# One wide matmul for both parts of x: the joint product in the feature-major steps of a two-block network

## The chip, the cores and the metric

The kernel runs on one core of one Trainium2 chip. The metric is the device time of one execution in microseconds (us). Three runs of the kernel before took 2135.95, 2133.17 and 2133.64 us, median 2133.64. The profiled execution is a fourth one.

## The reference

Two blocks of two layers each work on 256 tokens of 1024 features, in float32. Cut to what matters here:

```
h = layer_norm(x)
for layer in 0, 1:                                   # first block
    proj = h @ w_in[layer]                           # 1024 -> 2048: pool input, q, k, v
    mix  = concat(pool_mixer(...), stick_breaking_attention(q, k, v)) @ w_out
    h    = layer_norm(ALPHA * h + mix)
    f    = swiglu(h) if layer == 0 else top2_of_8_experts(h)
    h    = layer_norm(ALPHA * h + f)
for layer in 0, 1:                                   # second block
    z   = rms_norm(x) @ w_in_2[layer]                # gated recurrence, 3 groups of attention, gates
    x   = x + (gated mix of both branches) @ w_out_2
    x   = x + square(relu(rms_norm(x) @ w_up_2)) @ w_down_2
return rms_norm(x)
```

`swiglu(x) = (silu(x @ wg) * (x @ wu)) @ wd`, with an inner width of 2816; the inner width of the last pair is 4096.

## The kernel before

**Two parts of every number.** TensorE works here on float32 numbers that are rounded to fewer bits (the type fp32r). To keep the accuracy, every operand is a sum of two such numbers, a high part and a low part: `xh`, `xl` for the activations, `whi`, `wlo` for the weights. A product is then three matmuls, whi·xh + whi·xl + wlo·xh (`mm3`, L216 to L227). The product of the two low parts is left out.

**The stream of weights.** All weights come in units of 128 partitions by 2048 numbers (1 MB), in the order in which they are used. A unit is loaded by SyncE's DMA queue into `raw` (`emit_dma`, L144), then `emit_split` makes its two parts: ScalarE writes the high part (`whi`, L166, 2048 columns), VectorE subtracts it from `raw` for the low part (`wlo`, L168, one instruction over 2048 columns). `take` hands out the next unit, and keeps three units split and eight or so loaded ahead. `raw`, `whi` and `wlo` come out of one pool of 13 slots, so a new `whi` can wait for the slot of a unit that TensorE is just done with. There is a second way to make the low part: for units at or behind `self.hold` it is cut into three pieces of 592, 784 and 672 columns (L176), which are put into a list, `self.fill`, and are emitted one at a time by `filler`.

**Two ways to multiply.** A product whose result has tokens on the partitions (`chunk_tok`, `tok_part`, the experts, `down`) holds x still and moves 512 columns of weights (L225 to L227). A product whose result has features on the partitions holds 128x128 weights still and moves the 256 tokens of x (L221 to L223). The second kind is `chunk_feat` (L275). One call makes 512 features: two units (j), four columns blocks of 128 features (c), four steps of the contraction (k), so 32 steps of three matmuls of 256 columns. Its results lie in two of the four PSUM banks of the pool `acc`, two blocks c to a bank, so that a call and the next one use different banks. When both units are done, ScalarE or VectorE takes the results out of PSUM, 512 columns at a time.

**Who calls it.** 44 calls of `chunk_feat`, 1408 steps:

- the mixer of the first block, twice per layer (q and k): 4
- the dense feed-forward network of layer 0 (`ffn`, L725), one for each 256 inner features but the first 256: 10
- the second block (`second`, L1115), per layer: one for the forget gates, one for the queries of the recurrence, six for queries and keys of the three attention groups: 16
- the "up" half of the second block's feed-forward network, per layer: 7, so 14

**Side work.** `pump` runs the next piece of each generator in `self.side` behind every second block c, so four times in a call. Attention, pooling and the recurrence (`hgrn`) are such generators. A piece puts matmuls on TensorE's queue and their followers on ScalarE's and VectorE's. They use four other banks, two of them of the pool `ms`. Every engine works through its queue in the order in which the program put it there; nothing overtakes.

Where a stage ends, `boundary` normalises the two halves of the tokens and multiplies each by the next stage's first two units at once.

Of the kernel before, what the change touches and what calls it, by code (L numbers as in the profile page):

```python
# [10 lines left out]
F32 = mybir.dt.float32  # L11
# [86 lines left out]
class Net:  # L98
# [176 lines left out]
    def chunk_feat(self, x):  # L275

        xh, xl = x
        out = [self.bank(), self.bank()]
        for j in range(2):
            w = self.take(1)[0]  # L280
            for c in range(4):
                o = out[c // 2][:, (c % 2) * T:(c % 2 + 1) * T]
                for k in range(4):
                    kt = 4 * j + k
                    self.mm3(o, xh[:, kt, :], xl[:, kt, :], w[0][:, k, c * P:(c + 1) * P],
                             w[1][:, k, c * P:(c + 1) * P], kt == 0 and c % 2 == 0, kt == 7,
                             w_stationary=True, skip_group_check=True)
                if c % 2 == 1:
                    self.pump()
        return out  # L290
# [144 lines left out]
    def run(self, stop=None):  # L435
# [4 lines left out]
        self.x = (self.main.tile([P, KT, T], F32R, name="xh"), self.main.tile([P, KT, T], F32R, name="xl"))  # L440
# [160 lines left out]
    def mixer(self, l, ps):  # L601
# [3 lines left out]
        with self.mixs:  # L605
# [12 lines left out]
            for j in range(2):  # L618
                ps = self.chunk_feat(self.x)
                nc.scalar.activation(q[:, 2 * j:2 * j + 2].rearrange("p c t -> p (c t)"), ps[0], AF.Identity,  # L620
                                     scale=0.125)
                nc.vector.tensor_copy(k[:, 2 * j:2 * j + 2].rearrange("p c t -> p (c t)"), ps[1])
                for c in (2 * j, 2 * j + 1):
                    self.side.append(self.stick_pair(c, q, k, pairs, work))
# [100 lines left out]
    def ffn(self, ps):  # L725
        nc, a, tc = self.nc, self.a, self.tc
        with tc.tile_pool(name="ffn", bufs=1) as pool, tc.tile_pool(name="ffnw", bufs=2) as work:
# [13 lines left out]
            self.side.append(first())  # L741
            for j in range(1, FF // 256):
                ps2 = self.chunk_feat(self.x)
                s = work.tile([P, 512], F32, name="s")
                nc.scalar.activation(s, ps2[0], AF.Silu)
                nc.vector.tensor_mul(s, s, ps2[1])
                h, l = (m[:, 2 * j:2 * j + 2].rearrange("p c t -> p (c t)") for m in hid)
                nc.scalar.activation(h, s, AF.Identity)
                nc.vector.tensor_sub(l, s, h.bitcast(F32))
# [136 lines left out]
    def experts(self, gate, rank, xt, rest, iota1, sums, end):  # L886
        nc, a, tc = self.nc, self.a, self.tc
        mm = nc.tensor.matmul
        with tc.tile_pool(name="moew", bufs=2) as work:
# [4 lines left out]
            def gather(p):  # L894
# [7 lines left out]
                for i in range(2):  # L902
                    for k in range(0, KT, 2):
                        if p:
                            yield
                        ps = self.ms.tile([P, 512], F32, name="ms") if p else self.bank()
                        for j in range(2):
                            for t in range(2):
                                mm(ps[:, j * T:(j + 1) * T], xt[i][:, t, (k + j) * P:(k + j + 1) * P],
                                   s[:, t].rearrange("p e s -> p (e s)"), start=j == 0 and t == 0, stop=t == 1,  # L910
                                   skip_group_check=True)
                        nc.scalar.activation(xg[i][:, k:k + 2].rearrange("p k s -> p (k s)"), ps, AF.Identity)
# [202 lines left out]
    def second(self, l, ps, stop=None):  # L1115
        nc, a, tc = self.nc, self.a, self.tc
        self.n_ahead = N_AHEAD - 1
        with tc.tile_pool(name="z", bufs=1) as pool, tc.tile_pool(name="zw", bufs=2) as work:
# [12 lines left out]
            ps = self.chunk_feat(self.x)  # L1131
            for i in range(2):
                c = slice(512 * i, 512 * i + 512)
                nc.scalar.activation(f[:, c], ps[i], AF.Sigmoid)
                nc.scalar.activation(k[:, c], ps[i], AF.Sigmoid, scale=-1.0)
            for h in range(4):
                c = slice(T * h, T * h + T)
                nc.vector.tensor_scalar(f[:, c], f[:, c], lb[:, 4 + h:5 + h], lb[:, h:h + 1], op0=OP.mult, op1=OP.add)
                nc.vector.tensor_scalar(k[:, c], k[:, c], lb[:, 4 + h:5 + h], None, op0=OP.mult)
            ps = self.chunk_feat(self.x)  # L1140
            for i in range(2):
                c = slice(512 * i, 512 * i + 512)
                nc.scalar.activation(q[:, c], ps[i], AF.Sigmoid)
                nc.vector.tensor_mul(q[:, c], q[:, c], ps[i])
# [9 lines left out]
            for g in range(3):  # L1154
                qk = []
                for i in range(2):
                    ps = self.chunk_feat(self.x)
# [40 lines left out]
        with tc.tile_pool(name="up", bufs=1) as pool, tc.tile_pool(name="upw", bufs=2) as work:  # L1198
# [13 lines left out]
            self.side.append(first())  # L1212
            for j in range(1, FF2 // 512):
                ps2 = self.chunk_feat(self.x)
                for i in range(2):
                    s = work.tile([P, 512], F32, name="s")
# [3 lines left out]
                    nc.scalar.activation(h, s, AF.Identity)  # L1220
                    nc.vector.tensor_sub(lo, s, h.bitcast(F32))
# [218 lines left out]
```

## Time and profile before

| | |
|---|---|
| median of the runs | 2133.64 us (2133.17 to 2135.95) |
| profiled execution, its own time | 2134.69 us |
| its span, first to last instruction | 2132.9 us |
| TensorE busy / its weight loads | 2104.6 us (99%) / 1824.6 us (86%) |
| VectorE / ScalarE / GpSimd busy | 1484.9 us (70%) / 1215.3 us (57%) / 76.6 us (4%) |
| mean granted TensorE clock | 0.994 of full speed |
| HBM read | 503.73 MB, 237 GB/s over the span |

The busy time of a matmul in the profile is longer than the time after which the next one starts (a 256-column one is 0.28 us long, and the next starts 0.12 us after it), so the rate is read from the starts in the timeline. TensorE is named PE there, its weight loads PEld, VectorE DVE, ScalarE ACT and GpSimd POOL. L and a number is a line of the kernel.

### The profile page before, as it was taken

The page shows a single profiled execution, that of the slowest core. Times are in us where ns is not written, and L with a number is a line of the kernel's source. Part 1 is how long each engine was busy: PE and PEld are TensorE (multiplying, and loading weights), DVE is VectorE, ACT ScalarE, POOL GpSimd, SP SyncE. Part 2 cuts the span into 40 slices and gives each one's busy share as a digit, 9 for nine tenths or more (in the row PEclk, how much of TensorE's full clock was granted, in tenths as well). Part 3 has the DMA queues.
Part 4 walks back from the last instruction along what each step waited for, and adds up shares of the span by engine and source line. Part 5 has one row for each costly group of instructions (what it writes and reads, how often), then busy time and mean ns, then how long its engine had stood idle before and what let it go on. Part 6 is the DMA issues. An engine that isn't in the chain of part 4 may idle for free. (4 is left out here: it accounts for less than half of the span.)

```text
span 2132.9 us, 28748 instructions
## 1 busy us (share of the span) xinstructions
PE 2104.6 (99%) x11853; PEld 1824.6 (86%) x11853; DVE 1484.9 (70%) x1308; ACT 1215.3 (57%) x1191; POOL 76.6 (4%) x88
## 2 busy tenths in 40 slices
PE   9999999999999999999999899999999999999998
PEld 7899988788888888888888799988998899988987
DVE  6465454798888989898898666667654566666643
ACT  4544446677777777777776535464543444555542
POOL 0000000000000000000000110200000011100000
PEclk9999999899999999999999999999999999999999
DMA  8275555699999999999998354444654654436551
GB/s 302 88 246 181 197 186 189 223 362 369 363 345 367 369 344 352 375 365 336 371 358 304 139 176 149 137 147 156 221 196 152 221 171 145 144 124 225 185 197 60
DMA packets 240510, 508.29 MB, mean 238 GB/s; under 512 B 9346, under 2 KB 57346, under 8 KB 240372
## 3 DMA queue, kind: packets, MB, share of 16 engines
q1 hardware_dynamic: 237120, 497.22, 67.4%
q0 software_dynamic: 2816, 8.56, 1.4%
q8 instruction: 95, 1.56, 0.3%
q10 hardware_dynamic: 436, 0.60, 0.1%
q14 instruction: 43, 0.35, 0.0%
HBM read 503.73 MB, written 1.05 MB: 237 GB/s over the span
## 5 line engine op out<-in xcount | busy, mean ns | idle before, releaser
L168 DVE TENSOR_TENSOR wlo<-raw,whi 128x2048 fp32r<-128x2048 f32 x463 | 1061.0, 2294 | 367.9 <-ACT whi L166 318.6
L166 ACT ACTIVATE whi<-raw 128x2048 fp32r<-128x2048 f32 x467 | 886.9, 1915 | 259.1 <-PE acc L226 81.6
L225 PE MATMUL acc<-whi,xh 128*128 128x512 f32 x1168 | 467.1, 400 | 2.2 <-ACT xh L350 2.1
L227 PE MATMUL acc<-whi,xl 128*128 128x512 f32 x1168 | 458.2, 392 | 0.5 <-DVE xl L351 0.5
L226 PE MATMUL acc<-wlo,xh 128*128 128x512 f32 x1168 | 456.3, 391 | 1.6 <-DVE wlo L163 0.9
L221 PE MATMUL acc<-xh,whi 128*128 128x256 f32 x1408 | 403.8, 287 | 0.0
L223 PE MATMUL acc<-xh,wlo 128*128 128x256 f32 x1408 | 398.3, 283 | 0.0
L222 PE MATMUL acc<-xl,whi 128*128 128x256 f32 x1408 | 398.2, 283 | 0.0
L225 PE MATMUL acc<-whi,hidh 128*128 128x512 f32 x696 | 272.7, 392 | 0.0
L226 PE MATMUL acc<-wlo,hidh 128*128 128x512 f32 x696 | 271.2, 390 | 0.0
L227 PE MATMUL acc<-whi,hidl 128*128 128x512 f32 x696 | 271.0, 389 | 0.0
L221 PEld LDWEIGHTS acc<-xh,whi 128*128 128x128 f32 x1408 | 269.9, 192 | 1.3
L222 PEld LDWEIGHTS acc<-xl,whi 128*128 128x128 f32 x1408 | 270.0, 192 | 0.7
L223 PEld LDWEIGHTS acc<-xh,wlo 128*128 128x128 f32 x1408 | 269.8, 192 | 0.0
L227 PEld LDWEIGHTS acc<-whi,xl 128*128 128x128 f32 x1168 | 219.7, 188 | 52.7 <-DVE xl L351 5.9
L225 PEld LDWEIGHTS acc<-whi,xh 128*128 128x128 f32 x1168 | 220.2, 189 | 47.9 <-ACT xh L350 5.3
L226 PEld LDWEIGHTS acc<-wlo,xh 128*128 128x128 f32 x1168 | 220.3, 189 | 46.1 <-DVE wlo L163 1.9
L227 PEld LDWEIGHTS acc<-whi,hidl 128*128 128x128 f32 x696 | 130.6, 188 | 27.8
L225 PEld LDWEIGHTS acc<-whi,hidh 128*128 128x128 f32 x696 | 130.8, 188 | 25.9
L226 PEld LDWEIGHTS acc<-wlo,hidh 128*128 128x128 f32 x696 | 130.8, 188 | 25.6
L350 ACT ACTIVATE xh<-tr 128x512 fp32r<-128x512 f32 x40 | 22.5, 596 | 77.8 <-PE tr L357 77.6
L970 ACT ACTIVATE hidh<-tr 128x512 fp32r<-128x512 f32 (+1 forms) x48 | 27.1, 564 | 64.3 <-PE tr L357 64.3
(313 smaller groups left out, 1607.6 us busy)
## 6 DMA issues: line engine op xcount, KB each, us to landing
raw<-in_moe_wd_dram SPq DMA_DIRECT2D x88, 1024.0 KB, 6.5
raw<-in_moe_wg_dram SPq DMA_DIRECT2D x80, 1024.0 KB, 7.0
raw<-in_moe_wu_dram SPq DMA_DIRECT2D x80, 1024.0 KB, 6.6
raw<-in_w_in_dram SPq DMA_DIRECT2D x74, 1024.0 KB, 5.5
raw<-in_w_up_dram SPq DMA_DIRECT2D x32, 1024.0 KB, 5.4
raw<-in_w_down_dram SPq DMA_DIRECT2D x32, 1024.0 KB, 5.0
raw<-in_w_out_dram SPq DMA_DIRECT2D x16, 1024.0 KB, 5.3
raw<-in_ffn_wg_dram SPq DMA_DIRECT2D x22, 512.0 KB, 4.2
```

What stands on the lines that cost most here:

```text
L166: self.nc.scalar.activation(hi, raw, AF.Identity)
L168: self.nc.vector.tensor_sub(lo, raw, hi.bitcast(F32))
L221: mm(out, wh, xh, start=start, stop=False, **kw)
L222: mm(out, wh, xl, start=False, stop=False, **kw)
L223: mm(out, wl, xh, start=False, stop=stop, **kw)
L225: mm(out, xh, wh, start=start, stop=False, **kw)
L226: mm(out, xh, wl, start=False, stop=False, **kw)
L227: mm(out, xl, wh, start=False, stop=stop, **kw)
L350: self.nc.scalar.activation(h, v, AF.Identity)
L970: nc.scalar.activation(h[:, :n], v, AF.Identity)
```

## The change

`chunk_feat` is replaced by `chunk_join`. The high and the low part of x now lie side by side in one tile `xx`, so that one matmul of 512 columns makes whi·xh into the first and whi·xl into the second half of a bank, and a second one of 256 columns adds wlo·xh to the second half. A block c has a bank of its own, and a call uses all four banks. The two halves are added when they leave PSUM: ScalarE copies the first half (256 columns), VectorE adds the second (`joined`).

In these calls the low parts of the weights are made in the three pieces (hold is 0 around `take`). What `fill` holds is emitted at the first unit; the pieces of the second unit's `take` come one ahead of each block's exit from PSUM. What follows the exit (silu, square, gates) is handed on as a function, and is emitted behind the next block's exit. At the start of both feed-forward networks the first piece of the generator `first` runs at once instead of at the next `pump`.

```diff
-    def chunk_feat(self, x):
-        xh, xl = x
-        out = [self.bank(), self.bank()]
+    def chunk_join(self, sink):
+        mm = self.nc.tensor.matmul
+        out = []
         for j in range(2):
+            hold, self.hold = self.hold, 0
             w = self.take(1)[0]
+            self.hold = hold
+            if j == 0:
+                self.after()
+                self.filler(len(self.fill))
             for c in range(4):
-                o = out[c // 2][:, (c % 2) * T:(c % 2 + 1) * T]
+                if j == 0:
+                    out.append(self.bank())
                 for k in range(4):
                     kt = 4 * j + k
-                    self.mm3(o, xh[:, kt, :], xl[:, kt, :], w[0][:, k, c * P:(c + 1) * P],
-                             w[1][:, k, c * P:(c + 1) * P], kt == 0 and c % 2 == 0, kt == 7,
-                             w_stationary=True, skip_group_check=True)
+                    cw = slice(c * P, (c + 1) * P)
+                    mm(out[c], w[0][:, k, cw], self.xx[:, kt].rearrange("p i t -> p (i t)"), start=kt == 0, stop=False,
+                       skip_group_check=True)
+                    mm(out[c][:, T:], w[1][:, k, cw], self.xx[:, kt, 0], start=False, stop=kt == 7,
+                       skip_group_check=True)
+                if j == 1:
+                    self.filler()
+                    late = sink(c, (out[c][:, :T], out[c][:, T:]))
+                    self.after()
+                    self.late = late
                 if c % 2 == 1:
                     self.pump()
-        return out
+        self.filler(len(self.fill))
+
+    def after(self):
+        late, self.late = self.late, None
+        if late is not None:
+            late()
+
+    def joined(self, dst, halves, scale=1.0):
+        self.nc.scalar.activation(dst, halves[0], AF.Identity, scale=scale)
+        if scale == 1.0:
+            self.nc.vector.tensor_add(dst, dst, halves[1])
+        else:
+            self.nc.vector.scalar_tensor_tensor(dst, halves[1], scale, dst, op0=OP.mult, op1=OP.add)
...
-        self.x = (self.main.tile([P, KT, T], F32R, name="xh"), self.main.tile([P, KT, T], F32R, name="xl"))
+        self.xx = self.main.tile([P, KT, 2, T], F32R, name="xx")
+        self.x = (self.xx[:, :, 0], self.xx[:, :, 1])
+        self.late = None
...
@@ the queries and keys of an attention group @@
-                    ps = self.chunk_feat(self.x)
+                    x = pool.tile([P, 4, T], F32, name="qa" if i == 0 else "ka", bufs=2)
+
+                    def sink(c, ps, x=x):
+                        self.joined(x[:, c], ps)
+
+                    self.chunk_join(sink)
                     if i == 1:
                         self.rotate(*qk[0], rope)
-                    x = pool.tile([P, 4, T], F32, name="qa" if i == 0 else "ka", bufs=2)
-                    for j in range(2):
-                        nc.scalar.activation(x[:, 2 * j:2 * j + 2].rearrange("p c t -> p (c t)"), ps[j], AF.Identity)
...
@@ the up half of the second block's feed-forward network @@
-            self.side.append(first())
+            f = first()
+            next(f)
+            self.side.append(f)
             for j in range(1, FF2 // 512):
-                ps2 = self.chunk_feat(self.x)
-                for i in range(2):
-                    s = work.tile([P, 512], F32, name="s")
-                    nc.scalar.activation(s, ps2[i], AF.Relu)
-                    nc.vector.tensor_mul(s, s, ps2[i])
+                s = []
+
+                def square(i, j=j, s=s):
+                    v = s[i]
+                    nc.vector.scalar_tensor_tensor(v, v, 0.0, v, op0=OP.max, op1=OP.mult)
                     h, lo = (m[:, 4 * j + 2 * i:4 * j + 2 * i + 2].rearrange("p c t -> p (c t)") for m in hid)
-                    nc.scalar.activation(h, s, AF.Identity)
-                    nc.vector.tensor_sub(lo, s, h.bitcast(F32))
+                    nc.scalar.activation(h, v, AF.Identity)
+                    self.fill.insert(1, lambda: nc.vector.tensor_sub(lo, v, h.bitcast(F32)))
+
+                def sink(c, ps, s=s, square=square):
+                    if c % 2 == 0:
+                        s.append(work.tile([P, 512], F32, name="s"))
+                    self.joined(s[-1][:, c % 2 * T:c % 2 * T + T], ps)
+                    return (lambda: square(c // 2)) if c % 2 else None
+
+                self.chunk_join(sink)
+            self.after()
+            self.filler(len(self.fill))
...
```

The other callers change in the same manner: the dense network gets a silu and a product as late functions, the recurrence its gates and its swish, the mixer's q and k are only joined. In the experts one copy is written as a pattern of 2 x 256 columns instead of 512.

**Where the order moves.** The first place is VectorE in the up half, layer 0 of the second block, second call. `s` is the result outside PSUM (two tiles by turns), `acc` a bank, `hidl` and `hidh` the parts of the squared result. Before:

```order
L168 TENSOR_TENSOR wlo_15058<-raw_14915,whi_15057 128x2048
L168 TENSOR_TENSOR wlo_15112<-raw_14917,whi_15111 128x2048
L1218 TENSOR_TENSOR s_15165<-s_15165,acc_15055 128x512
L1221 TENSOR_TENSOR hidl_14908<-s_15165,hidh_14907 128x512
L1218 TENSOR_TENSOR s_15170<-s_15170,acc_15056 128x512
L1221 TENSOR_TENSOR hidl_14908<-s_15170,hidh_14907 128x512
```

The same place in the changed kernel, from the second unit of the call on:

```order
L176 TENSOR_TENSOR wlo_14674<-raw_14514,whi_14673 128x592
L315 TENSOR_TENSOR s_14687<-s_14687,acc_14637 128x256
L176 TENSOR_TENSOR wlo_14674<-raw_14514,whi_14673 128x784
L315 TENSOR_TENSOR s_14687<-s_14687,acc_14646 128x256
L176 TENSOR_TENSOR wlo_14674<-raw_14514,whi_14673 128x672
L315 TENSOR_TENSOR s_14710<-s_14710,acc_14655 128x256
L1275 SCALAR_TENSOR_TENSOR s_14687<-s_14687 128x512
L1278 TENSOR_TENSOR hidl_14502<-s_14687,hidh_14501 128x512
L315 TENSOR_TENSOR s_14710<-s_14710,acc_14664 128x256
L1275 SCALAR_TENSOR_TENSOR s_14710<-s_14710 128x512
```

Four adds over 256 columns (L315) have come in between the pieces of the low part, and the fourth stands behind the square and the low part of the first half.

The second place is VectorE in the first unit of the query call of the second attention group (g = 1, layer 0). `att` is the recurrence's matrix, copied out of a bank of the pool `ms`; `w` holds the scores' maxima. Before:

```order
L168 TENSOR_TENSOR wlo<-raw,whi 128x2048
L1295 COPY_PREDICATED att_12887<-lev,ms 128x32x8
L1365 TENSOR_REDUCE w_13357<-ms 128x2
L1366 TENSOR_SCALAR w_13357<-w_13357 128x2
L1371 COPY ma<-w_13357 128x2
```

After:

```order
L176 TENSOR_TENSOR wlo<-raw,whi 128x592
L176 TENSOR_TENSOR wlo<-raw,whi 128x784
L176 TENSOR_TENSOR wlo<-raw,whi 128x672
L1362 COPY_PREDICATED att_12596<-lev,ms 128x32x8
L1432 TENSOR_REDUCE w_13026<-ms 128x2
```

Here only the low part is in pieces; the copy that frees the bank still stands behind all of it.

## Rows read from the trace of the kernel before

**Rows 1.** The page, parts 1 and 2: busy time, granted clock.

```profile
span 2132.9 us, 28748 instructions
PE 2104.6 (99%) x11853; PEld 1824.6 (86%) x11853; DVE 1484.9 (70%) x1308; ACT 1215.3 (57%) x1191; POOL 76.6 (4%) x88
PEclk9999999899999999999999999999999999999999
```

**Rows 2.** Waits of TensorE, longest first: us in total, times, longest us.

```profile
PE tr L418 <- DVEq L869: 4.0, 1, 4.0
PE tr L357 <- DVE r L432: 3.5, 2, 2.8
```

**Rows 3.** Windows, three calls: us; busy PE, PEld, DVE, ACT, POOL; clock; DMA; GB/s.

```profile
155.40:166.92 11.52, 11.52 (x99) 11.52 (x98) 5.97 (x4) 4.95 (x4) 0.00 (x0) 1.00 0.59 183
...
1358.43:1374.77 16.34, 16.34 (x137) 15.97 (x135) 9.42 (x19) 8.94 (x27) 3.62 (x5) 1.00 0.41 134
1515.52:1527.04 11.52, 11.52 (x99) 11.52 (x98) 7.28 (x7) 6.18 (x6) 0.00 (x0) 1.00 0.62 188
```

**Rows 4.** Timeline, TensorE, one call of the dense network: start, us, instruction.

```profile
155.40 0.28 PE L221 MATMUL acc<-xh,whi 128*128 128x256 f32 x1
...
166.92 0.28 PE L221 MATMUL acc<-xh,whi 128*128 128x256 f32 x1
```

**Rows 5.** Timeline, TensorE, 512-column matmuls of a token-major product, then a call.

```profile
1340.54 0.39 PE L225 MATMUL acc<-whi,xh 128*128 128x512 f32 x1
...
1341.90 0.28 PE L221 MATMUL acc<-xh,whi 128*128 128x256 f32 x1
```

**Rows 6.** Timeline, TensorE, among the experts: 256 columns between 512 and 512.

```profile
589.39 0.39 PE L227 MATMUL acc<-whi,hidl 128*128 128x512 f32 x1
589.62 0.64 PE L909 MATMUL ms<-slots,xtl 128*128 128x256 f32 x4
590.09 0.40 PE L225 MATMUL acc<-whi,hidh 128*128 128x512 f32 x1
```

**Rows 7.** The page, part 5: count, busy us, mean ns, idle before.

```profile
L221 PE MATMUL acc<-xh,whi 128*128 128x256 f32 x1408 | 403.8, 287 | 0.0
```

**Rows 8.** Groups by line and shape: count, busy us, mean ns, idle before.

```profile
L168 DVE TENSOR_TENSOR wlo<-raw,whi 128x2048 fp32r<-128x2048 f32 x463 | 1061.0, 2294 | 367.9 <-ACT whi L166 318.6 <-PE acc L226 22.5 <-issue 9.0
L166 ACT ACTIVATE whi<-raw 128x2048 fp32r<-128x2048 f32 x467 | 886.9, 1915 | 259.1 <-PE acc L226 81.6 <-PE acc L227 69.3 <-DVE wlo L168 57.5
L1218 DVE TENSOR_TENSOR s<-s,acc 128x512 f32<-128x512 f32 x28 | 19.1, 683 | 2.6 <-ACT s L1217 2.6
L1220 ACT ACTIVATE hidh<-s 128x512 fp32r<-128x512 f32 x28 | 17.7, 632 | 30.5 <-DVE s L1218 30.5
L991 DVE TENSOR_TENSOR hs<-hs,acc 128x256 f32<-128x256 f32 x8 | 3.3, 410 | 0.0
L989 ACT ACTIVATE hs<-acc 128x256 f32<-128x256 f32 x8 | 3.0, 376 | 0.0
```

**Rows 9.** One line, L176: the pieces; ns min/median/max, starts, forms.

```profile
L176 DVE TENSOR_TENSOR wlo<-raw,whi x6: 766/849/966, 402.8 to 1193.5; 128x592 fp32r<-128x592 f32 x2, 128x784 fp32r<-128x784 f32 x2, 128x672 fp32r<-128x672 f32 x2
```

**Rows 10.** Timeline, ScalarE in the up half; in brackets the idle time and what ended it.

```profile
1521.47 1.91 ACT L166 ACTIVATE whi<-raw 128x2048 fp32r<-128x2048 f32 x1 [1.91 <-PE acc L223]
```

**Rows 11.** Timeline, VectorE and TensorE, first unit of the group-1 query call.

```profile
1302.70 2.29 DVE L168 TENSOR_TENSOR wlo<-raw,whi 128x2048 fp32r<-128x2048 f32 x1 [5.77 <-ACT whi L166]
...
1304.91 0.42 DVE L1295 COPY_PREDICATED att<-lev,ms 128x256 f32<-128x256 uint8 x1
...
1305.39 1.10 PE L1292 MATMUL ms<-A,B 128*128 128x64 f32 x8
```

**Rows 12.** Timeline, the same engines, first unit of the group-2 key call.

```profile
1361.22 2.29 DVE L168 TENSOR_TENSOR wlo<-raw,whi 128x2048 fp32r<-128x2048 f32 x1 [1.82 <-ACT whi L166]
...
1364.98 1.12 DVE L1335 SCALAR_TENSOR_TENSOR y<-ms,rr,og 128x128 f32<-128x128 f32 x4 [1.16 <-POOL rr L1332]
...
1366.22 0.60 PE L357 MATMUL tr<-mats,y 128*128 128x128 f32 x4
```

More of the change, by code (lines that the diff above doesn't have):

```diff
@@ L739, in first, with silu, product, sink @@
                     self.split_to(hid, self.transpose4(hs[t], 2), 0, t, 2)
-            self.side.append(first())
+            f = first()
+            next(f)
+            self.side.append(f)
             for j in range(1, FF // 256):
-                ps2 = self.chunk_feat(self.x)
-                s = work.tile([P, 512], F32, name="s")
-                nc.scalar.activation(s, ps2[0], AF.Silu)
-                nc.vector.tensor_mul(s, s, ps2[1])
-                h, l = (m[:, 2 * j:2 * j + 2].rearrange("p c t -> p (c t)") for m in hid)
-                nc.scalar.activation(h, s, AF.Identity)
-                nc.vector.tensor_sub(l, s, h.bitcast(F32))
+                gs, us = (work.tile([P, 512], F32, name=n) for n in ("s", "u"))
+                def silu(s=gs):
+                    nc.scalar.activation(s, s, AF.Silu)
+                def product(j=j, s=gs, u=us):
+                    h, l = (m[:, 2 * j:2 * j + 2].rearrange("p c t -> p (c t)") for m in hid)
+                    nc.vector.tensor_mul(s, s, u)
+                    nc.scalar.activation(h, s, AF.Identity)
+                    self.fill.insert(1, lambda: nc.vector.tensor_sub(l, s, h.bitcast(F32)))
+                def sink(c, ps, gs=gs, us=us, late=(None, silu, None, product)):
+                    self.joined((us if c > 1 else gs)[:, c % 2 * T:c % 2 * T + T], ps)
+                    return late[c]
+                self.chunk_join(sink)
                 if j == 6:
                     g, b = self.load_rows((a["ln2_g"][0], a["ln2_b"][0]))
+            self.after()
+            self.filler(len(self.fill))
             acc = self.down(hid, FF // P)
@@ L911, in gather @@
                                    skip_group_check=True)
[L912 removed]
+                        nc.scalar.activation(xg[i][:, k:k + 2], ps.rearrange("p (k s) -> p k s", k=2), AF.Identity)
             def turn(p):
@@ L1130, in second, with gates, swish, sink @@
             f = pool.tile([P, 4 * T], F32, name="C")
-            ps = self.chunk_feat(self.x)
-            for i in range(2):
+            sq = pool.tile([P, 4 * T], F32, name="D")
+            def gates(i):
                 c = slice(512 * i, 512 * i + 512)
[L1134 to L1141, printed above, removed]
-                c = slice(512 * i, 512 * i + 512)
-                nc.scalar.activation(q[:, c], ps[i], AF.Sigmoid)
-                nc.vector.tensor_mul(q[:, c], q[:, c], ps[i])
+                nc.scalar.activation(k[:, c], f[:, c], AF.Sigmoid, scale=-1.0)
+                nc.scalar.activation(f[:, c], f[:, c], AF.Sigmoid)
+                for h in (2 * i, 2 * i + 1):
+                    c = slice(T * h, T * h + T)
+                    nc.vector.tensor_scalar(k[:, c], k[:, c], lb[:, 4 + h:5 + h], None, op0=OP.mult)
+                    nc.vector.tensor_scalar(f[:, c], f[:, c], lb[:, 4 + h:5 + h], lb[:, h:h + 1], op0=OP.mult,
+                                            op1=OP.add)
+            def swish(i):
+                c = slice(512 * i, 512 * i + 512)
+                nc.scalar.activation(sq[:, c], q[:, c], AF.Sigmoid)
+                self.fill.insert(1, lambda: nc.vector.tensor_mul(q[:, c], q[:, c], sq[:, c]))
+            for dst, then in ((f, gates), (q, swish)):
+                def sink(c, ps, dst=dst, then=then):
+                    self.joined(dst[:, c * T:c * T + T], ps)
+                    return (lambda: then(c // 2)) if c % 2 else None
+                self.chunk_join(sink)
+            self.after()
+            self.filler(len(self.fill))
             og = pool.tile([P, 2, 512], F32, name="og")
@@ L1210, in first @@
                     self.split_to(hid, self.transpose4(hs[t]), 0, t)
-            self.side.append(first())
+            f = first()
+            next(f)
+            self.side.append(f)
             for j in range(1, FF2 // 512):
-                ps2 = self.chunk_feat(self.x)
-                for i in range(2):
-                    s = work.tile([P, 512], F32, name="s")
-                    nc.scalar.activation(s, ps2[i], AF.Relu)
-                    nc.vector.tensor_mul(s, s, ps2[i])
-                    h, lo = (m[:, 4 * j + 2 * i:4 * j + 2 * i + 2].rearrange("p c t -> p (c t)") for m in hid)
-                    nc.scalar.activation(h, s, AF.Identity)
-                    nc.vector.tensor_sub(lo, s, h.bitcast(F32))
+                s = []
+                def square(i, j=j, s=s):
+                    v = s[i]
+                    nc.vector.scalar_tensor_tensor(v, v, 0.0, v, op0=OP.max, op1=OP.mult)
+                    h, lo = (m[:, 4 * j + 2 * i:4 * j + 2 * i + 2].rearrange("p c t -> p (c t)") for m in hid)
+                    nc.scalar.activation(h, v, AF.Identity)
[5 more added lines that the diff above has]
+                    return (lambda: square(c // 2)) if c % 2 else None
+                self.chunk_join(sink)
+            self.after()
+            self.filler(len(self.fill))
             acc3 = self.down(hid, FF2 // P)
```

7 lines of the change are left out of this document (3 added, 4 removed).

## The prediction

> **What bounds the kernel now.** I began with the page's busy times and its line of granted clocks [rows 1]: TensorE is busy for 99% of the span, with the granted clock at nine tenths or full speed in every slice, while VectorE is at 70% and ScalarE at 57%. Next the waits of TensorE, the longest of which are 4.0 and 3.5 us [rows 2]: idle time can hardly be won here, only shorter matmul work. Next the windows [rows 3], since the change touches one kind of stage: a call of the dense network (first row) and one of the up half (last row) each have 11.52 us of TensorE work in 11.52 us, at clock 1.00, with a DMA share of 0.59 and 0.62 and VectorE at 5.97 and 7.28 us. So these calls are bound by TensorE, and neither the weights' transfer nor another engine stands close behind. Then the timeline of TensorE, from which the pace comes [rows 4 to 6]; the groups, for the durations on ScalarE and VectorE [rows 8, 9]; and last the places where side work leaves little room [rows 10 to 12].
>
> **The pace of a matmul.** A call starts at 155.40 and the next at 166.92 [rows 4]: 11.52 us for 96 matmuls of 256 columns, 0.1200 us each. Six matmuls of 512 columns go from 1340.54 to 1341.90 [rows 5]: 0.2267 us each. So two of 256 cost 0.2400 where one of 512 costs 0.2267, and what a matmul costs beside its columns is 2 × 0.1200 − 0.2267 = 0.0133 us. The question is whether this holds where the two widths alternate, as they will. Among the experts they do once [rows 6]: a 512-column one from 589.39 to 589.62 (0.23), four of 256 from 589.62 to 590.09 (0.47, or 0.118 each), then 512 again. No width pays for its neighbour there beyond the timeline's rounding. I take 0.2267 + 0.1200 = 0.3467 us for a step that took 0.3600.
>
> **What it removes.** Each step loses one matmul and 0.0133 us. The count of steps is that of L221, 1408 [rows 7]: 1408 × 0.0133 = 18.8 us. A call falls from 11.52 to 11.09 us. Columns and products are the same as before.
>
> **What it adds, and what hides it.** Per call, from [rows 8, 9]:
> - VectorE, low parts: a whole one is 2.29 us, three pieces 0.77 + 0.97 + 0.85 = 2.58. Two units: 5.17 where it was 4.59.
> - VectorE, four adds of 256 columns from a bank: 0.41 each, by the nearest row, L991: 1.64.
> - VectorE in the up half keeps its two squares (0.68 by L1218, which had the same width) and two low parts (0.68 likewise): 2.73. Together 9.54 of 11.09 us, 86%. The dense network: 5.97 + 0.58 + 1.64 = 8.2.
> - ScalarE: two high parts of 1.92, four copies of 256 columns at 0.38 (L989), two of 512 at 0.63 (L1220): 6.6 of 11.09.
>
> None of it is on TensorE, which is the cover. The cover is gone when a bank comes free too late: a call takes all four banks, so the next one's block c0 needs the first bank at once, c1 four steps (4 × 0.3467 = 1.39 us) later, and so on. A block is finished in the second unit, and its bank is needed again 12 steps, 4.16 us, after that: c0 is done 1.39 us after the half and needed at the end of the call.
>
> I walk through the up half, the heaviest. The high part of the second unit is what starts late: in the call that starts at 1515.52 ScalarE waits 1.91 us for TensorE (the slot of an older unit) and starts at 1521.47, when half the call is over [rows 10]. In the new call the half is at 5.55 us and that start at some 5.74, its end at 7.65. Then the first piece on VectorE to 8.42, and behind it the rest:
> - c0: done by TensorE at 6.93, copied 7.65 to 8.03, added by 8.83; needed at 11.09. Slack 2.3 us.
> - c1: the piece of 784 to 9.8, add by 10.2; needed at 12.48. Slack 2.3.
> - c2: the piece of 672, add by 11.45; needed at 13.87. Slack 2.4.
> - c3: done at 11.09; square, ScalarE's part, copy and add before it on VectorE: free by 13.9; needed at 15.25. Slack 1.35 us.
>
> The high part and the pieces are for units that `take` splits three ahead, so their lateness isn't waited for in the same call. I cost all this at nothing; if the cover of 1.35 to 2.4 us is gone, TensorE stops for what is lacking, at each of the calls concerned.
>
> Edits that I cost at nothing together: the tile in which x's parts lie side by side (the writers have the same shapes), the experts' copy in a pattern of 2 × 256, and the first exit pieces at the start of both feed-forward networks (their exits come one block sooner, ahead of the next high part, and their data have been finished by the previous stage). Bounds for the three together: the longest waits of the trace on either side, −4 to +4 us [rows 2]; the value nearest the rows is 0, as TensorE's queue keeps its order there.
>
> **What it costs at side work.** Where a generator's next matmul waits for VectorE, the longer low part goes straight onto TensorE's path. In the group-1 query call the low part starts at 1302.70, behind it the copy that frees a bank starts at 1304.91 and takes 0.42, and TensorE uses that bank at 1305.39 [rows 11]: 1305.33 against 1305.39, a slack of 0.06 us. In the changed kernel the three pieces end 0.29 later, and TensorE is there some 16 steps × 0.0133 = 0.21 sooner: a new wait of 0.29 + 0.21 − 0.06 = 0.44 us. In the group-2 key call the chain of low part (from 1361.22), gates and y (1364.98 + 1.12 = 1366.10) meets a transpose at 1366.22 [rows 12], a slack of 0.12: a wait of some 0.4. Two layers have both: 2 × (0.44 + 0.4) = 1.7 us. The whole window of recurrence and attention around it (second row of rows 3) has VectorE at 9.42 of 16.34 us, so elsewhere it has room; I allow 0.3 us for the rest, 2.0 in all. Bounds: from 0 (a pump that comes a little later takes the wait away) to twice that in each of the 12 attention calls, 12 × 0.88 = 10.6 us. I take 2.0, as only these two places stand within 0.3 us.
>
> **The sum.** The profiled execution took 2134.69 us, 1.8 of it outside the span, which nothing here touches. 2134.69 − 18.8 + 2.0 = 2117.9 us. The runs' median, 2133.64, is 1.05 below the profiled execution: 2116.8 us.
>
> **The rivals.**
>
> A, the forecast: 2116.8 us, its own range 2114 (no new stall) to 2121 (three times the stalls).
>
> B, late banks take part back. For it: VectorE rises to 86% in the up half, c3 has 1.35 us, and the recurrence and attention put their own pieces between. Against it: the walk above, and 8.2 of 11.09 in the dense network. If the 12 attention calls and the 14 up calls lose 0.3 us each on average, that is 7.8 us: some 2124.6, range 2121 to 2129.
>
> C, the pace doesn't change: 768 columns cost 0.3600 whichever way they are cut, because the alternating widths are each paced by something that isn't the columns (the weight load, say, which is busy for all of 11.52 us in a call [rows 3]). Then only the 2.0 us of stalls are left: 2135.6, within the noise. Against it: rows 6. The Trainium skill has a rule near it: "TensorE: Matmul & The Clock Gate", section "Back-to-back issue gap", gives the isolated gap at full clock as the columns over 2.4 GHz plus 2.5 ns. By that rule, and as an estimate, one matmul less saves 2.5 ns a step, 3.5 us in all, and the time would be 2132. The trace disagrees: 0.1200 and 0.2267 us leave 13 ns beside the columns, and the measurement decides.
>
> D, slower: the next call's first step waits for c0's add. All four banks are in use, so there is no spare one, as there was with two of four; if the second unit's high part comes later than the walk has it, or VectorE's queue is filled by side work, c0 is added after 11.09 us and each us of delay is a us of TensorE, in 44 calls. The gain of 0.43 us a call is gone at a delay of 0.43, and from 0.53 us on the kernel is slower by over 0.2%. With 1.0 us: 2133.6 + 44 − 18.8 = 2158.8 us. For it: ScalarE waits for a slot in each such call [rows 10]. Against it: c0 has 2.3 us.
>
> E, a larger gain: what a matmul costs beside its columns is its weight load, and behind a 512-column one the next load has long been done. Then the 256-column one saves its 13 ns too, the step is 0.3333, and 1408 × 0.0267 = 37.5 us go: 2134.69 − 37.5 + 2.0 − 1.05 = 2098. For it: the weight load's 100% in [rows 3]. Against it: from 589.39 to 590.09 one of 512 and four of 256 took 0.70 where the two paces give 0.71 [rows 6], which is the rounding of the timeline, and no 13 ns are plain in it. The same section of the Trainium skill says that in a stream of loads and matmuls both set the spacing; no row here separates them.
>
> **How the numbers follow.** Chances: A 0.76, B 0.11, C 0.04, D 0.05, E 0.04. I call no change what lies within 0.2% (4.3 us), which is about what this measurement can tell. A, B and E are faster: 0.91, less 0.01 for the end of B's range. C is the same, with that 0.01. D is slower. The range goes from 2112.5 (A with no stall, and the edits costed at nothing giving back 1.6 us) to 2128.0 (most of B); E, C and D lie outside with 0.13, and an end of B.
>
> **What would show it.** In the changed profile the matmuls of a step should start 0.227 and 0.120 us apart and a plain call should last 11.09 us; 0.36 a step would be C, 0.333 would be E. The chain from c0's copy and add to the next call's first matmul should show no idle time of TensorE; one with VectorE's add as its releaser would be B or D. VectorE should be at 9.5 us in an up call, and its pieces at 0.77, 0.97 and 0.85. In the query call of group 1 and the key call of group 2 TensorE should wait for VectorE for about 0.4 us each. Stages that don't use these calls should last as long as before. The forecast is wrong if idle time of TensorE in the 44 calls is above 7 us, or if the step isn't near 0.347 us.

## The result: slower, by 25 us

The changed kernel takes 2158.92 us (median of four, 2157.35 to 2159.37), the kernel before beside it 2134.05: a ratio of 1.0115, with a 95% interval from 1.0102 to 1.0127. The forecast was 2116.8 us, with a range to 2128. The profiled execution took 2158.73 us, with a span of 2156.9.

### The profile page after: what moved, and what is told of

Same layout as the page of the kernel before. It is cut to its first block, busy times and chain, and to the rows that moved or that the text cites. A ratio compares the mean times of both kernels' runs of the same rounds, so it can differ in the third digit from the quotient of the medians.

```text
span 2156.9 us, 26392 instructions
## 1 busy us (share of the span) xinstructions
PE 2101.8 (97%) x10445; PEld 1745.8 (81%) x10445; DVE 1558.7 (72%) x1656; ACT 1242.3 (58%) x1311; POOL 76.4 (4%) x88
## 5 line engine op out<-in xcount | busy, mean ns | idle before, releaser
L168 DVE TENSOR_TENSOR wlo<-raw,whi 128x2048 fp32r<-128x2048 f32 x375 | 861.6, 2301 | 224.1 <-ACT whi L166 177.2
L166 ACT ACTIVATE whi<-raw 128x2048 fp32r<-128x2048 f32 x467 | 887.2, 1915 | 234.7 <-PE acc L226 74.2
L294 PE MATMUL acc<-xx,whi 128*128 128x512 f32 x1408 | 506.6, 402 | 21.5 <-DVE s L315 20.0
L225 PE MATMUL acc<-whi,xx 128*128 128x512 f32 x1168 | 466.7, 400 | 2.2 <-ACT xx L377 2.1
L227 PE MATMUL acc<-whi,xx 128*128 128x512 f32 x1168 | 458.0, 392 | 0.5 <-DVE xx L378 0.5
L226 PE MATMUL acc<-wlo,xx 128*128 128x512 f32 x1168 | 456.1, 390 | 1.6 <-DVE wlo L163 0.9
L296 PE MATMUL acc<-xx,wlo 128*128 128x256 f32 x1408 | 394.3, 280 | 0.0
L294 PEld LDWEIGHTS acc<-xx,whi 128*128 128x128 f32 x1408 | 264.4, 188 | 91.9 <-DVE s L315 29.7
L176 DVE TENSOR_TENSOR wlo<-raw,whi 128x592 fp32r<-128x592 f32 (+2 forms) x270 | 230.5, 875 | 145.9 <-ACT whi L166 51.9
L296 PEld LDWEIGHTS acc<-xx,wlo 128*128 128x128 f32 x1408 | 265.8, 189 | 0.7
L227 PEld LDWEIGHTS acc<-whi,xx 128*128 128x128 f32 x1168 | 219.6, 188 | 52.9 <-DVE xx L378 6.1
L225 PEld LDWEIGHTS acc<-whi,xx 128*128 128x128 f32 x1168 | 220.0, 188 | 48.0 <-ACT xx L377 5.3
L226 PEld LDWEIGHTS acc<-wlo,xx 128*128 128x128 f32 x1168 | 220.1, 188 | 45.9 <-DVE wlo L163 1.9
```

The costliest lines, as they stand in the source:

```text
L166: self.nc.scalar.activation(hi, raw, AF.Identity)
L168: self.nc.vector.tensor_sub(lo, raw, hi.bitcast(F32))
L176: self.fill.append(lambda c=c: self.nc.vector.tensor_sub(lo[:, c], raw[:, c], hi[:, c].bitcast(F32)))
L225: mm(out, xh, wh, start=start, stop=False, **kw)
L226: mm(out, xh, wl, start=False, stop=False, **kw)
L227: mm(out, xl, wh, start=False, stop=stop, **kw)
```

## The profile after

The page, parts 1 and 2, answers to [rows 1]:

```profile
span 2156.9 us, 26392 instructions
PE 2101.8 (97%) x10445; PEld 1745.8 (81%) x10445; DVE 1558.7 (72%) x1656; ACT 1242.3 (58%) x1311; POOL 76.4 (4%) x88
PEclk9999999899999999999999999999999999999999
```

The granted clock is what it was. TensorE has 1408 matmuls less and is busy 97% where it was 99%. The waits of TensorE, longest first (answering to [rows 2]), begin with one that wasn't there:

```profile
PE acc L294 <- DVE s L315: 20.0, 22, 1.5
PE tr L445 <- DVEq L911: 4.1, 1, 4.1
```

Windows over a call of the dense network and one of the up half (columns as in [rows 3], first and last row):

```profile
156.21:167.52 11.31, 11.31 (x66) 9.81 (x65) 7.58 (x12) 6.18 (x8) 0.00 (x0) 1.00 0.61 185
...
1520.38:1533.48 13.10, 11.76 (x64) 9.75 (x64) 8.77 (x15) 6.18 (x8) 0.00 (x0) 1.00 0.48 158
```

The dense call fell from 11.52 to 11.31 us, not to 11.09; the up call rose to 13.10. By the starts of the calls in the two timelines the 24.0 us of the span divide so: the 14 up calls +21.4, the ten calls of the dense network +4.2 (of which its first and its last four are some 1.0 us longer each, the others 0.1 or 0.2 shorter), the 16 calls of the second block's first half -3.9, the mixer's four -1.1, all the rest +3.3.

Where the up call loses its time stands on TensorE at the end of that call (timeline; in brackets the idle time and what ended it):

```profile
1531.83 0.40 PE L294 MATMUL acc<-xx,whi 128*128 128x512 f32 x1
1532.07 0.28 PE L296 MATMUL acc<-xx,wlo 128*128 128x256 f32 x1
1533.48 0.50 PE L294 MATMUL acc<-xx,whi 128*128 128x512 f32 x1 [1.14 <-DVE s L315]
```

The next call's first matmul starts 1.41 us after the last one of this call, where 0.12 is usual: it waits for c0's add (L315), as in rival D. The same delay shows at the ends of all 14 up calls and of five dense ones, where the next start comes 1.3 to 1.65 us later than usual. In most up calls c3's block then starts late too (0.4 to 0.5 us behind c2's last matmul), so that such a call lasts 1.8 us longer than a plain dense one. But why is c0's add late? VectorE and ScalarE in the second half of the same call:

```profile
1526.73 1.92 ACT L166 ACTIVATE whi<-raw 128x2048 fp32r<-128x2048 f32 x1 [0.23 <-PE acc L296]
1528.55 0.36 ACT L313 ACTIVATE s<-acc 128x256 f32<-128x256 f32 x1
```

```profile
1527.96 1.74 DVE L176 TENSOR_TENSOR wlo<-raw,whi 128x784 fp32r<-128x784 f32 x2
1532.32 0.77 DVE L176 TENSOR_TENSOR wlo<-raw,whi 128x592 fp32r<-128x592 f32 x1 [2.62 <-ACT s L313]
1533.01 0.41 DVE L315 TENSOR_TENSOR s<-s,acc 128x256 f32<-128x256 f32 x1
```

The high part is ready at 1528.65 and c0's copy at 1528.91. Still VectorE stands idle for 2.62 us ahead of the piece of 592 columns, until 1532.32, just behind TensorE's last matmul with the running unit's high part (the L294 above, 1531.83 + 0.40 = 1532.23). (The releaser named, L313, had ended at 1531.35 with c2's copy: a case of an engine that had long been done.) The view of line L176 shows that wait by itself, as a waiting instruction of VectorE's queue that starts at 1526.8 and lasts 5.47 us, until 1532.27:

```profile
L176 DVEq EVENT_SEMAPHORE  x2: 1609/3538/5468, 1525.0 to 1526.8; - x2
```

So the piece waits for neither of its inputs but for the place of its output. The pool of 13 places (slots) also holds rows of norm factors and the running sums, so weights have 11 of them in the up half. (In the dense network the rows come behind the sixth call, and its last four calls are slow.) In the built program the places are given out like this. Counted are the low parts whose place still belongs to the unit that TensorE is working with when the low part is emitted, of 20 units in the dense network and 14 in each up half:

```
kernel                          dense network   up, layer 0   up, layer 1
before                                0              0             0
changed                               9             14            14
pieces alone (e7)                     8             14            14
exits ahead of pieces (e3)            9             14            14
whole low parts (e2)                  0              0             0
one transfer fewer ahead (e1)         0              1             1
two fewer in the up half (e13)        0              0             0
```

A low part that is made later asks later for its place; the transfer of a unit further ahead takes the free one, and the piece gets the place of the running unit's high part. For the second unit of a call that comes free when the call ends (for the first one at the call's half). c0's add stands behind the piece on VectorE, and TensorE behind the add.

## Experiments

All times are medians; e1 to e4 and e5 to e8 were run beside the kernel before at 2134.12 and 2133.81, e9 to e12 at 2134.55, e13 and e14 at 2132.85.

**e1, e8: one transfer fewer ahead.** In both feed-forward networks, around the calls:

```diff
+            self.n_ahead -= 1
             for j in range(1, FF2 // 512):
...
+            self.n_ahead += 1
             acc3 = self.down(hid, FF2 // P)
```

> One transfer of weights fewer is started ahead in the calls of both feed-forward networks (7 units ahead, not 8), nothing else. Theory S (slot): in the slow calls the first piece of the second unit's low part waits for a place in the weight pool, which only comes free when the running unit is used up at the end of the call; c0's add stands behind it on VectorE and the next call's first matmul behind that. With a slot more, 14 of the 19 or so waits of 1.2 to 1.8 us go: the up calls fall from 13.1 to 11.3 us, the last ffn calls from 12.5 to 11.3, the time to 2128 to 2132 us. Rival V (VectorE has too much to do: adds and pieces): the queue is as full as before, the up calls stay at 13.1 us, the time at 2159.

2126.50 us, ratio 0.9965 [0.9952, 0.9977], a little below the expected range, since many calls lasted 11.09 us and not 11.3. The place is the cause: the calls' excess goes with the waits for it, while the queue of VectorE holds the same work. Of the 20.0 us for which TensorE waited for those adds (L315), this is left:

```profile
PE acc L294 <- DVE s L315: 2.5, 3, 1.1
```

In an up call of e1 the piece now starts behind its high part, the idle time is 1.48 us and ends on L166, and c0's add is done 2.5 us ahead of its need (the call ends at 1544.26):

```profile
1540.64 0.78 DVE L176 TENSOR_TENSOR wlo<-raw,whi 128x592 fp32r<-128x592 f32 x1 [1.48 <-ACT whi L166]
1541.34 0.42 DVE L315 TENSOR_TENSOR s<-s,acc 128x256 f32<-128x256 f32 x1
```

**e12: the same edit in the kernel before.**

> A control: the kernel before with one transfer fewer ahead in the feed-forward calls, nothing else. If the shorter lead only gives the changed kernel a place in the pool, it is worth nothing here: 2132 to 2136. If it is a gain of its own (less traffic at once), 2127 to 2130, and the first run's gain is not the joined product's.

2133.56 us, ratio 0.9996 [0.9987, 1.0006]: worth nothing by itself.

**e2: the low part whole.** `chunk_join` without the two lines on `hold`.

> The joint product stays, but the low part is made by one instruction, emitted when the unit is taken, as in the kernel before. Theory S: the low part asks for its place early and gets a free one, so the up calls last 11.3 us and the time is 2126 to 2132. Rival V: VectorE has 0.6 us less a call, so the wait of 1.4 us shrinks to 0.8 us at most: up calls 12.5 us, time about 2148.

2130.87 us, ratio 0.9984 [0.9974, 0.9993]. The big wait is gone, but five of the seven up calls of a layer last 12.06 to 12.11 us, not 11.3: with the place free, a low part of 2.29 us in one piece holds up c0's add, and a call's first matmul starts 0.7 to 0.9 us later than usual. Rival V has that much in it; the pieces do serve their purpose.

**e3: the exit ahead of the piece.**

```diff
-                    self.filler()
                     late = sink(c, (out[c][:, :T], out[c][:, T:]))
+                    self.filler()
```

> Each block's exit from the bank is emitted ahead of the piece, not behind it; the pieces and the places in the weight pool are as in the changed kernel. Theory S, in its order part: the wait for the place is still there, until the end of the call, but c0's add no longer stands behind it; c1's add then comes some 1.3 us after the end of the call, just when its bank is needed (1.41), so most of the stall goes: up calls 11.3 to 11.7 us, time 2129 to 2136. Rival V: the same work in VectorE's queue; c0's add comes one piece (0.8 us) sooner, the others as late as before: up calls 12.3 us, time about 2146.

2140.91 us, between the two: c0 is in time though the wait for the place stays, the dense calls run at 11.09 us, but in the up half c3, which I had not reckoned, comes 1.0 us late (12.26 to 12.50 us in all calls but the first). That is near the rival's 12.3, but for another reason, and neither forecast of the time held.

**e7, e11: the pieces alone, in the kernel before.** e11 also runs `next(f)` ahead of the calls, as the change does.

```diff
+            hold, self.hold = self.hold, 0
             w = self.take(1)[0]
+            self.hold = hold
+            if j == 0:
+                self.filler(len(self.fill))
...
+                if j == 1:
+                    self.filler()
...
+        self.filler(len(self.fill))
```

> The kernel before with one part of the change: the low parts in three pieces in chunk_feat, behind the blocks of the second unit; the matmuls, banks and exits are those of before. Theory S: VectorE waits for the place in the weight pool until the end of the call here too, but two of the four banks are free then, so TensorE waits for nothing: 11.52 us a call, 2133 to 2138. Rival: the late low part is itself what stops TensorE (its unit is wanted): up calls above 12.5 us, time 2150 or more.

2148.39 us. The calls in the steady state last 11.52 us, as theory S has it: with two banks spare the same wait doesn't stop TensorE. But the first up call of each layer was 5 us longer, which it hadn't said. There the wait shows at its longest on VectorE, and the exits of the stage's first bank, hence four transposes, stood behind it:

```profile
1499.45 0.78 DVE L176 TENSOR_TENSOR wlo<-raw,whi 128x592 fp32r<-128x592 f32 x1 [5.32 <-PE acc L222]
```

> As the run of the pieces alone, in the kernel before's matmuls, but the exits of the stage's first bank are emitted before the first call, as in the changed kernel. In the pieces' run the up calls lasted 11.52 us, but the first of each layer 5 us more: the first bank's exits stood on VectorE behind a piece that waited for its place, and TensorE's transposes behind those. If that is all, the 10 us go: 2138. If the exits behind the pieces cost elsewhere too, it stays at 2143 to 2148.

2139.07 us; the later up calls last 11.52 us and the first of each layer 12.38, as in the kernel before: that was it for the 10 us. The run is still 4.5 us slower than the kernel before; 1.8 of them are the mixer's second calls (15.05 us for 14.15), the others weren't followed up. The wait for the place is harmful wherever something urgent stands behind it.

**e6: three narrow matmuls into the new banks**, with e1's edit.

```diff
-                    mm(out[c], w[0][:, k, cw], self.xx[:, kt].rearrange("p i t -> p (i t)"), start=kt == 0, stop=False,
+                    for i in range(2):
+                        mm(out[c][:, i * T:(i + 1) * T], w[0][:, k, cw], self.xx[:, kt, i], ...
```

> As the first run (one transfer fewer ahead), but each step is three matmuls of 256 columns as in the kernel before, into the same four banks with the same exits. This takes the wide matmul away and leaves the rest. Theory: without the slot's wait the banks and exits cost little, so the steps at 0.360 us give the time before and the few waits at side work: 2134 to 2138. Rival: the gain of the first run came with the exits or the order of the work, not with the wide matmul: 2127.

2140.60 us: without the wide matmul the change costs 6.8 us, which is more than expected; 3.4 of them lie in the first two up calls of each layer, where a place is still short in e1 too. The wide matmul itself is worth 2140.6 - 2126.5 = 14.1 us, which is 10.0 ns a step, where 13.3 were forecast.

**e4, e5: the wide matmuls of a block first**, then the four narrow ones; e4 on the changed kernel, e5 with e1's edit.

> Within each block the four 512-column matmuls come first and then the four of 256, in place of turns; the waits stay. Theory P (pace): each change of width costs about 7 ns (a step took 0.3534 us where 0.2267 + 0.1200 = 0.3467 was forecast), so one change in four steps saves 3 x 6.7 ns = 20 ns a block, 352 blocks, 7 us: a plain ffn call goes from 11.31 to 11.14 us, the time from 2159 to about 2152. Rival: the 0.3534 is what 768 columns with two weight loads cost in any order: 2159.

> The two edits together: one transfer fewer ahead in the feed-forward calls, and within each block the four 512-column matmuls ahead of the four of 256. If the two act on different things (a place in the pool; the pace) their gains add: 2126.5 by the first, 7.5 us by the second (2158.9 to 2151.4): 2119. If the wait left over by the first hides in the second, or the pace of the first (347 ns a step in ffn, already) leaves nothing to group, 2124 to 2127.

2151.36 and 2127.22 us: it gains 7.6 us on the one and nothing on the other. A call without waits takes 11.20 to 11.23 us in that order (350 or 351 ns a step); a step in turns takes 353 or 347. Theory P, a price for each change of width, is refuted: 347 with a change at every matmul is less than 350 with a quarter of them.

**Two paces of one program.** e8 was e1's kernel again.

> The first run's kernel once more, for a second profile. Its steps took 347 ns in the ffn calls and in the up calls of layer 1, and 353 in those of layer 0, though the program is the same. If the pace hangs on the program (places in memory, order), each stage shows the same pace again; if it hangs on how a stretch begins, as the flips after waits suggest, some stages show the other one. Time 2126.5 either way, within 3 us.

2126.82 us. In e1 the later up calls took 11.31 us in layer 0 and 11.09 in layer 1, in e8 it was the other way round. Windows of e1 over a dense call and an up call of either layer, then of e8 over the same two up calls; the granted clock is the same in all, and weight loads and VectorE are alike in the up calls:

```profile
165.35:176.44 11.09, 11.09 (x66) 9.79 (x65) 7.84 (x12) 6.19 (x8) 0.00 (x0) 1.00 0.64 191
1532.96:1544.26 11.30, 11.30 (x66) 9.81 (x65) 8.76 (x15) 6.18 (x8) 0.00 (x0) 1.00 0.56 186
1985.55:1996.64 11.09, 11.09 (x66) 9.78 (x65) 8.77 (x15) 6.18 (x8) 0.00 (x0) 1.00 0.61 191
```

```profile
1532.99:1544.09 11.10, 11.10 (x67) 9.79 (x66) 8.79 (x15) 6.18 (x8) 0.00 (x0) 1.00 0.58 189
1985.31:1996.62 11.31, 11.31 (x67) 9.81 (x65) 8.78 (x15) 6.18 (x8) 0.00 (x0) 1.00 0.59 188
```

In every profile with steps in turns a pace, once there, lasts until TensorE is interrupted, by a stop or by other matmuls. A stretch that begins right behind 512-column matmuls of a token-major product begins at 353; behind the transposes in the first call of both feed-forward networks it was 347 each time; behind a stop for a bank it is one or the other.

**e9: the narrow matmul first in each step**, with e1's edit.

> The first run's kernel (one transfer fewer ahead) with the two matmuls of a step in the other order: 256 columns of the low part first, then the 512. Theory: a stretch keeps the pace (347 or 353 ns a step) that its beginning gave it, and beginning with the narrow one behind a 512-column product changes that: if the calls that begin so (the first of ffn, of the gates, of up) then run at 347 from the start, the 353 stretches of the second block's first half go: 16 calls x 0.21 = 3.4 us, and time 2122 to 2124. If the pace is drawn by other things: 2125 to 2130, with both paces in the profile.

2125.36 us; the stretches of the second block still begin at 353, so it isn't the order that sets the pace there.

**e10: the low parts whole in the mixer, exits first in the up half**, with e1's edit.

> The first run's kernel with two more edits: in the mixer's calls the low part is whole again, and in the up calls each block's exit stands ahead of the piece. By the profiles of the second and third run the first up call then loses 1.3 us of waits in each layer (2.6) and the gap behind the mixer's first call 0.7 in each layer (1.4, of which 0.4 stays as other waits): 2126.5 - 2.6 - 1.0 = 2123. If the exits in that order delay the pieces so that a later unit is late, 2126 or more.

2125.81 us. The first up call of each layer falls from 13.31 to 12.01 us, but the second one rises to 12.39 (11.81 and 11.68 in e1): exits first moves half of the wait. All later up calls ran at the slower pace here, in both layers, which takes back another 1.1 us against e1.

**e13: no place short; e14: one small matmul more.** e13 is e9's kernel with whole low parts in the mixer and two transfers fewer ahead in the up half. e14 adds

```diff
+                if touch and j == 0 and c == 0:
+                    d = self.ms.tile([P, 512], F32, name="ms")
+                    mm(d[:, :64], w[0][:, 0, :P], self.xx[:, 0, 0, :64], start=True, stop=True)
```

behind the first block of the forget gates' call.

> The swapped order (256 columns first), low parts whole in the mixer's calls, and two transfers fewer ahead in the up calls (one in ffn). Theory S: in the run with one fewer the second unit of the first up call still found no place and cost 1.0 us in the first two up calls of each layer; with two fewer no low part waits for a unit in use, so the first two up calls fall to the others' length: 2 x 1.0 us; with the mixer's 1 us: 2125.4 - 3 = 2122.4. All later up calls should be at 347 ns a step, since nothing stops TensorE after the first call's transposes. Rival: the shorter lead makes TensorE wait for weights, 2126 or more.

2121.28 us, ratio 0.9947 [0.9933, 0.9960]. The plain up calls of both layers last 11.09 us, the first of each, which has side matmuls, 0.35 less than before; a window over one:

```profile
1507.70:1518.79 11.09, 11.09 (x66) 9.78 (x65) 8.94 (x15) 6.19 (x8) 0.00 (x0) 1.00 0.59 189
```

No low part waits for a unit in use, and this is faster than both kernels.

> As the run beside it, with one matmul of 64 columns more (its result is read by nobody) behind the first block of the forget gates' call in both layers. That call and the next ran at 353 ns a step from their first step to their last in every profile. If an interruption alone sets the pace, both go to 347 behind it: 2 x 60 steps x 6.7 ns = 0.8 us less, less the added matmul (0.06 to 0.1 us each), and the pace is seen in the profile whatever the time says. If the pace hangs on what the call computes or where its data lie, it stays at 353.

2120.93 us, ratio 0.9946 [0.9930, 0.9961]; the time is not told apart from e13's, the pace is. TensorE in e14 at that place: a pair of steps takes 0.71 us ahead of the small matmul.

```profile
1203.26 0.40 PE L296 MATMUL acc<-xx,whi 128*128 128x512 f32 x1
...
1203.97 0.40 PE L296 MATMUL acc<-xx,whi 128*128 128x512 f32 x1
...
1204.56 0.19 PE L305 MATMUL ms<-xx,whi 128*128 128x64 f32 x1
1204.59 0.37 PE L294 MATMUL acc<-xx,wlo 128*128 128x256 f32 x1
```

Behind it the steps of this call and of the next take 347 ns, in both layers. The next call in e13, then in e14:

```profile
1214.48:1225.78 11.30, 11.30 (x65) 9.80 (x64) 8.27 (x17) 8.55 (x12) 0.00 (x0) 1.00 0.60 190
```

```profile
1214.38:1225.47 11.09, 11.09 (x65) 9.78 (x64) 8.03 (x17) 8.34 (x12) 0.00 (x0) 1.00 0.61 191
```

So neither what the call computes nor where its data lie fixes the pace, and an interruption alone can change it. It doesn't always give the faster one: behind the stops for a bank both came. What in TensorE holds a pace was not tried and stays open.

## Why the prediction was wrong

- **The step that failed** is the walk through the up half, "Then the first piece on VectorE to 8.42". I started the piece when its high part was ready and gave its output a place for nothing. The piece started 11.9 us into the call, at its end, because its place was the running unit's, and the call behind it started 1.3 to 1.65 us late, 19 times (14 up calls, five dense ones). One transfer fewer ahead (e1) gave 32 us back. That places were short stood in the prediction itself: by [rows 10] ScalarE's high part stood 1.91 us for a slot, so no free one was left. In a full pool a later request isn't served as the earlier one was: it gets the place of another unit. The rest of the walk holds: where the place is free (e1), c0's slack is 2.5 us (forecast 2.3) and c3's add (1534.67 to 1535.09 in the call from 1532.96, needed 4.2 us into it) has 2.1 (forecast 1.35).
- **Rival D** named the right wait and, by chance, the right time. Its cause was wrong, a late high part or a full queue: the high part was in time and the queue idle. Its price was 1.0 us in 44 calls; it was 1.3 to 1.65 in 19, and the smaller gain a step, the lost time at c3 and the rest made up the sum.
- **The gain per step** was mis-sized as well: 13.3 ns forecast, 6.6 at the slower pace, which held in most plain calls of the changed kernel. All 44 calls at 353 would save 9.3 us, not 18.8. The forecast 0.3467 is real, and in e13 most calls have it. The stretch among the experts in [rows 6] was too short to show either pace.
- **Adds, copies and pieces** cost 0.41, 0.37 and 0.78, 0.97, 0.88 us, as taken. VectorE in a call without waits is at 8.77 us (forecast 9.54): the durations of its instructions were added up, but those that follow each other directly overlap by 0.08 us (in e1's lines above the piece ends at 1541.42 and the add behind it starts at 1541.34).
- **Side work.** The group-1 query call waits for the copy of `att` for 0.4 us in each layer, as forecast (the waits of TensorE's weight loads show it: total, times, longest):

```profile
PEld ms L1359 <- DVE att L1362: 0.8, 2, 0.4
```

  In the group-2 key call no wait for `y` shows at the place forecast (it is ready at 1367.89, the transpose starts at 1367.96). The gap behind the mixer's first call, 0.7 us longer in each layer, was not foreseen; it goes with whole low parts (e2) and with the exits ahead of the pieces (e3).
- **Two slips in the working** on which nothing hangs: in [rows 1] one slice has the granted clock at eight tenths, not nine (none of the calls lies in it), and without new stalls the prediction's sum is 2114.8 us, not 2114.
- E is out: no step was near 333 ns. C is out: the wide matmul is worth 10 ns a step (e6).

## What to carry to other kernels

An instruction has three things to wait for: its inputs, its engine and the place of its output. Where a pool is so full that its tiles already wait for releases, moving a tile's first write later hands its place to whoever asks sooner, here the transfer ahead, and what stands behind that write in the queue pays. In the changed kernel a lead shorter by one unit gave back 32 us (e1), and in the kernel before it cost nothing (e12). And a pace of matmuls read from one width is a bound for a mixture, until a mixed stretch has been timed.

## What the runs showed of the hardware

A regular mixture of 512- and 256-column matmuls has two steady paces at the same granted clock of 1.00, 347 and 353 ns a step, which last for whole calls (11.09 and 11.30 us). One 64-column matmul between them turned the slower one into the faster, in both layers of e14.
